# The scaling of the next expert's gathered tokens, behind the Silu of the expert in front

## The chip, the cores and the metric

The kernel runs on one core of one Trainium2 chip. The metric is the device time of one execution in microseconds (us). Before the change it is 2817.28 us, the median of three runs (2815.06 to 2818.99). In what follows PE is TensorE, ACT the scalar engine, DVE VectorE, POOL GpSimd and SP SyncE; each works through its own list of instructions in order.

## The reference

One layer of an encoder: a mixer (windowed attention heads beside mLSTM heads), and behind it a routed mixture of 16 experts, each with the 128 tokens that it chooses among 1024. Only the mixture is touched here:

```python
def expert_choice_moe(h, w_router, w_gate, w_up, w_down):
    cap = CAPACITY_FACTOR * S // N_EXPERTS                 # 2 * 1024 // 16 = 128
    aff = jax.nn.softmax((h @ w_router).astype(jnp.float32), axis=-1)
    gates, idx = lax.top_k(jnp.swapaxes(aff, 1, 2), cap)
    xe = jax.vmap(lambda hb, ib: hb[ib])(h, idx)
    hid = jax.nn.silu(jnp.einsum('becd,edf->becf', xe, w_gate)) * jnp.einsum('becd,edf->becf', xe, w_up)
    ye = jnp.einsum('becf,efd->becd', hid, w_down) * gates[..., None].astype(h.dtype)
    ...
h2 = rms_norm(x) * (1 + sc2) + sh2
x = x + g2 * expert_choice_moe(h2, w_router, w_gate, w_up, w_down)
```

The model is 2048 wide and an expert 1024. All is float32.

## The kernel before

The experts run one after the other, e = 0 to 15, in the last two fifths of the execution. The kernel keeps the residual stream without its norm in HBM (x1p_d). So an expert's tokens are gathered by row (L1288), multiplied by 1/rms of their row (L1312, the scaling of which the change speaks: four pieces of 128x512 on ACT), transposed on PE in four groups of four 128x128 blocks (L1325), and given scale and shift of their column as they leave PSUM (L1334, four pieces per group into xtmp). Float32 accuracy is had from three products of fp32r: every operand is split into a rounded part and a rest. For tokens these are xh (L1337, ACT) and xl (L1338, DVE), for weights ehi (L1353, ACT) and elo (L1359, DVE).

Weights come in chunks of 1 MB over SP's queue, two blocks of 128x1024 in each. For every block ACT makes ehi (four buffers), DVE elo (three buffers), and PE does six matmuls of 128x512 (L419 with ehi, L420 with elo, L421 with the tokens' rest). An expert has 48 blocks: 16 of the gate matrix (g0 to g15), 16 of up (u0 to u15), 16 of down (d0 to d15). From expert 1 on they run in this order: g4 to g15 of expert e, u0 to u15 of e, g0 to g3 of expert e+1, d0 to d15 of e. The tokens of e+1 are made beside that: their transposes' groups 0 to 2 are issued from the up part on, group 3 behind g1. Group 0 is the operand of g0 to g3, group 1 that of g4 to g7, and so on.

Between gate and up stands the Silu (`gated`, L1385), which writes the first half of tile y (one buffer; the scatter of the expert before reads it). The product with up (`hidden`, L1391, DVE) fills the second half, is transposed (`hidden_T`, L1402) and split into hT (L1405, L1406). `down` scales the results into y (L1427) and scatters them with addition into the output (L1429, POOL).

The order on each engine isn't written out by hand alone. The code is written in one order, `issue_after` holds an instruction behind another, and a scheduler with a model of the times places what it may place. The step `prep` of expert e+1 (one-hot of the slots, positions, gather, 1/rms, scaling) is a generator that runs beside the gate part of expert e; nothing but data ties its scaling to a place in ACT's list.

Of the kernel before, what the change touches and what calls it, by code (L numbers as in the profile page):

```python
# [14 lines left out]
AF = mybir.ActivationFunctionType  # L15
# [71 lines left out]
def tile_kernel(ctx: ExitStack, tc: tile.TileContext, x, c, w_ada, b_ada, w_in, b_gates, q_gain, k_gain, sink,  # L87
                m_gain, w_out, w_router, w_gate, w_up, w_down, cosT, sinT, ident_in, near, after, out):
    nc = tc.nc
# [41 lines left out]
    def bank(tag="s", pool=None, dt=F32):  # L131
        pool = pool or (psA if tag == "acc" else psB)
        return pool.tile([128, 512], dt, name=tag, tag=tag)
# [787 lines left out]
    def order(e, w):  # L921
        return MIXED if e + w == 0 else PLAIN
# [349 lines left out]
    def prep(e, p):  # L1272
        oh = mo_p.tile([128, NT, 128], BF, name="oh")
        nc.vector.tensor_tensor(oh, iot[:, None, :].to_broadcast([128, NT, 128]),  # L1274
                                slot[:, :, e:e + 1].to_broadcast([128, NT, 128]), OP.is_equal)
        pm = bank("t")
        for i in range(NT):
            if e:
                nc.tensor.matmul(pm[:, 0:2], oh[:, i], place[:, i], start=i == 0, stop=i == NT - 1)
                continue  # L1280
            for j in range(2):
                nc.tensor.matmul(pm[:, 0:1], oh[:, i], place[:, i, j:j + 1], start=i + j == 0, stop=i + j == NT)
        mt = mo_p.tile([128, 12], F32, name="mt", bufs=3)
        idx = mo_p.tile([128, 1], I32, name="idx", bufs=3)
        xg = mo_p.tile([128, D], F32, name="xg")

        def gather(to, rows, at):
            return nc.gpsimd.indirect_dma_start(out=to, out_offset=None, in_=rows,  # L1288
                                                in_offset=bass.IndirectOffsetOnAxis(ap=at[:, :1], axis=0))

        if e:
            nc.vector.tensor_copy(mt[:, 0:2], pm[:, 0:2])
            p["at"] = nc.vector.tensor_add(idx, mt[:, 0:1], mt[:, 1:2])
            p["fetch"] = gather(xg, x1p_d, idx)
        else:

            for q in FIRST_Q:
                at = mo_p.tile([128, 1], I32, name=f"idx{q}")
                nc.vector.tensor_scalar(at, pm[:, 0:1], 4.0, float(q), op0=OP.mult, op1=OP.add)
                p["fetch"] = gather(xg[:, q * 512:(q + 1) * 512], x1p_d.rearrange("t (q d) -> (t q) d", q=4), at)  # L1300
            p["at"] = nc.vector.tensor_copy(idx, pm[:, 0:1])
        yield
        pv = bank("t")
        for i in range(NT):
            nc.tensor.matmul(pv[:, 0:6], oh[:, i], info[:, i, e], start=i == 0, stop=i == NT - 1)
        nc.vector.tensor_reduce(mt[:, 9:11], pv[:, 0:6].rearrange("p (a b) -> p a b", a=2), axis=AX.X, op=OP.add)
        for i, q in enumerate(FIRST_Q if e == 0 else range(4)):
            xq = xg[:, q * 512:(q + 1) * 512]
            if e == 0 and i % 2:
                nc.vector.tensor_scalar(xq, xq, mt[:, 10:11], None, op0=OP.mult)  # L1310
            else:
                nc.scalar.mul(xq, xq, mt[:, 10:11])  # L1312
        p.update(mt=mt, idx=idx, xg=xg)
        yield

    def tokens_T(p, after=None, first=False):
        p["xh"], p["xl"], p["tmp"] = {}, {}, {}
        for q in FIRST_Q if first else range(4):
            xh = mo_p.tile([128, 4, 128], F32R, name=f"xh{q}")
            xl = mo_p.tile([128, 4, 128], F32R, name=f"xl{q}")  # L1320
            ps = bank("t")
            tmp = mo_p.tile([128, 512], F32, name="xtmp", bufs=2)
            with tc.issue_after(after.ins) if after else nullcontext():
                for b in range(4):
                    nc.tensor.transpose(ps[:, b * 128:(b + 1) * 128],  # L1325
                                        p["xg"][:, (4 * q + b) * 128:(4 * q + b + 1) * 128], ident)
            for b in range(4):
                k = 4 * q + b
                bs = slice(b * 128, (b + 1) * 128)
                if first and b % 2:  # L1330
                    nc.vector.tensor_scalar(tmp[:, bs], ps[:, bs], sc2x[:, k:k + 1], sh2x[:, k:k + 1],
                                            op0=OP.mult, op1=OP.add)
                else:
                    nc.scalar.activation(tmp[:, bs], ps[:, bs], AF.Identity, scale=sc2x[:, k:k + 1],  # L1334
                                         bias=sh2x[:, k:k + 1])
            t3 = tmp.rearrange("p (k n) -> p k n", k=4)
            nc.scalar.copy(xh, t3)  # L1337
            p["made"] = nc.vector.tensor_sub(xl, t3, xh)  # L1338
            p["xh"][q], p["xl"][q], p["tmp"][q] = xh, xl, tmp
            yield  # L1340
# [23 lines left out]
    def rows(e, p, w, cc, half, side):  # L1364

        if w not in p["acc"]:
            p["acc"][w] = [bank("acc") for _ in range(2)]
        acc, (first, last) = p["acc"][w], (order(e, w)[0], order(e, w)[-1])

        direct = e == 0 and (w, cc) in DIRECT  # L1370
        for j, hi, lo in chunk(e, w, cc, half, direct):
            start, stop = (cc, half) == first and j % 2 == 0, (cc, half) == last and j % 2 == 1
            for q in range(2):
                qs = slice(q * 512, (q + 1) * 512)
                if direct:
                    p["last"] = nc.tensor.matmul(acc[q], p["tmp"][cc][:, j * 128:(j + 1) * 128], hi[:, qs],
                                                 start=start, stop=stop)
                    continue
                p["last"] = mm3(acc[q], p["xh"][cc][:, j], p["xl"][cc][:, j], hi[:, qs], lo[:, qs], start, stop)
            side.step()  # L1380

    def gated(p):
        yt = p["y"] = mo_p.tile([128, D], F32, name="y", tag="y")
        for q in range(2):
            nc.scalar.activation(yt[:, q * 512:(q + 1) * 512], p["acc"][0][q], AF.Silu)  # L1385

    def hidden(p):
        yt, p["hid"] = p["y"], []
        for q in range(2):
            hid = yt[:, 1024 + q * 512:1024 + (q + 1) * 512]  # L1390
            nc.vector.tensor_mul(hid.rearrange("t (j p) -> t p j", j=4),  # L1391
                                 p["acc"][1][q].rearrange("t (p j) -> t p j", j=4),
                                 yt[:, q * 512:(q + 1) * 512].rearrange("t (p j) -> t p j", j=4))
            p["hid"].append(hid)
# [38 lines left out]
    first, side = Filler(), Filler()  # L1433
    nc.vector.tensor_reduce(slot[:, :, 0], cnt, axis=AX.X, op=OP.add)
    first.add(prep(0, P[0]))
    first.drain()
    first.add(tokens_T(P[0], first=True))
    first.drain()
    run(select(tp))
    for e in range(16):  # L1440
        p, nxt = P[e], P[e + 1] if e < 15 else None
        if nxt:
            side.add(prep(e + 1, nxt))
        for cc, half in order(e, 0):
            if e < 2 or cc:
                rows(e, p, 0, cc, half, side)
        gated(p)
        if e == 0:
            for cc, half in order(e, 1):
                rows(e, p, 1, cc, half, side)  # L1450
            side.drain()
            side.add(tokens_T(nxt, p["last"]))
            hidden(p)
            ht = hidden_T(p)
            for _ in range(2):
                side.step()
                next(ht)
            down(e, p, side)
            side.drain()
            continue  # L1460
        side.drain()

        turn = tokens_T(nxt) if nxt else iter(())
        for cc in range(4):
            for half in range(2):
                rows(e, p, 1, cc, half, side)
                if half == 0 and cc and nxt:
                    with tc.issue_after(used.ins):
                        next(turn)
            used = p["last"]  # L1470
        hidden(p)
        ht = hidden_T(p)
        if nxt:
            mid = Filler()
            mid.add(iter(()))
            rows(e + 1, nxt, 0, 0, 0, mid)
            with tc.issue_after(nxt["last"].ins):
                next(ht)
                next(ht)
                next(turn)  # L1480
            rows(e + 1, nxt, 0, 0, 1, mid)
        else:
            next(ht)
            next(ht)
        down(e, p, side)
# [45 lines left out]
```

## Time and profile before

| what | value |
|---|---|
| median of three runs | 2817.28 us |
| the profiled execution, and its span | 2817.95 us, 2816.24 us |
| PE busy | 2657.9 us (94%) |
| DVE busy | 2112.9 us (75%) |
| ACT busy | 1564.6 us (56%) |
| granted PE clock, mean | 0.974 |

The busy shares are means over the whole program; the experts are a stage of their own from about 1600 us on. The clock is a share of 2.4 GHz, so that 0.50 is the level of 1.2 GHz. The span is what the trace covers, the execution's time is a little longer.

### The profile page before, as it was taken

The numbers are of one execution on the slowest core, as the hardware profiler recorded it, in microseconds if no ns is written. First come the engines' busy times: TensorE is split into PE (matmuls) and PEld (weight loads), VectorE is DVE, ScalarE is ACT, GpSimd is POOL, SyncE is SP. The second block draws the span as 40 slices with busy tenths as digits, with TensorE's granted clock in tenths as the row PEclk, the third lists the DMA queues.
The fourth block names the chain that finished last, engine by engine and source line by source line (L and its number), as shares of the span: only waits on it lengthen the run. The fifth ranks groups of instructions, "written<-read, shape, count | busy, mean of one in ns | idle before, by whom it ended". The sixth has DMA issues, their size and how long they took to land. (4 is left out here: it accounts for less than half of the span.)

```text
span 2816.2 us, 36979 instructions
## 1 busy us (share of the span) xinstructions
PE 2657.9 (94%) x12392; PEld 2139.0 (76%) x12392; DVE 2112.9 (75%) x3507; ACT 1564.6 (56%) x2585; POOL 363.5 (13%) x311
## 2 busy tenths in 40 slices
PE   7998899999999999999999788999999999999997
PEld 6776787777777787777888566787777777777776
DVE  7777666666666665666745787899999889999886
ACT  6213332333343423333445457788888888888885
POOL 0000232000000003333444501100000000000000
PEclk9999999999999999999999899999999999999999
DMA  8874535555665556655497568999999999999993
GB/s 297 270 247 117 163 83 190 170 171 173 209 187 157 172 178 240 217 207 203 168 319 263 200 238 327 354 362 385 385 381 383 374 382 380 385 385 377 385 359 128
DMA packets 269559, 744.35 MB, mean 264 GB/s; under 512 B 29244, under 2 KB 83240, under 8 KB 232504
## 3 DMA queue, kind: packets, MB, share of 16 engines
q1 hardware_dynamic: 249192, 684.36, 67.6%
q0 software_dynamic: 4976, 33.64, 4.7%
q10 hardware_dynamic: 15200, 24.00, 2.3%
q8 instruction: 97, 1.59, 0.2%
q14 instruction: 94, 0.77, 0.1%
HBM read 672.01 MB, written 69.90 MB: 263 GB/s over the span
## 5 line engine op out<-in xcount | busy, mean ns | idle before, releaser
L1359 DVE TENSOR_TENSOR elo<-ew,ehi 128x1024 fp32r<-128x1024 f32 x432 | 507.6, 1220 | 49.1 <-ACT ehi L1353 35.9
L1353 ACT CAST ehi<-ew 128x1024 fp32r<-128x1024 f32 x432 | 445.1, 1059 | 89.9 <-PE acc L421 56.7
L1359 DVE TENSOR_TENSOR elo<-quad,ehi 128x1024 fp32r<-128x1024 f32 x324 | 380.9, 1219 | 51.9 <-ACT ehi L1353 43.6
L420 PE MATMUL acc<-elo,xh 128*128 128x512 f32 x1008 | 402.1, 399 | 9.7 <-DVE elo L1359 8.8
L421 PE MATMUL acc<-ehi,xl 128*128 128x512 f32 x1008 | 396.4, 393 | 0.0
L1353 ACT CAST ehi<-quad 128x1024 fp32r<-128x1024 f32 x324 | 335.1, 1059 | 72.0 <-PE acc L421 45.2
L419 PE MATMUL acc<-quad,w_hi 128*128 128x512 f32 x896 | 363.7, 407 | 7.3 <-ACT w_hi L388 4.1
L421 PE MATMUL acc<-quad,w_lo 128*128 128x512 f32 x896 | 357.8, 402 | 2.7 <-DVE w_lo L389 2.7
L420 PE MATMUL acc<-quad,w_hi 128*128 128x512 f32 x896 | 359.7, 401 | 0.0
L209 DVE SCALAR_TENSOR_TENSOR ada_acc<-ada_w,csil,ada_acc 128x512 f32<-128x512 f32 x360 | 273.3, 760 | 85.8 <-DMA ada_w<-in_w_ada_dram 82.3
L419 PE MATMUL acc<-ehi,xh 128*128 128x512 f32 x1008 | 322.8, 399 | 13.9 <-ACT ehi L1353 13.9
L388 ACT ACTIVATE w_hi<-w_raw,sc1p 128x128 fp32r<-128x128 f32 (+2 forms) x368 | 161.6, 491 | 312.8 <-PE acc L420 173.6
L420 PE MATMUL acc<-w_lo,quad 128*128 128x512 f32 x768 | 311.5, 406 | 6.7 <-DVE w_lo L378 5.5
L421 PE MATMUL acc<-w_hi,quad 128*128 128x512 f32 x768 | 306.1, 399 | 0.0
L419 PE MATMUL acc<-w_hi,quad 128*128 128x512 f32 x768 | 297.2, 414 | 6.6 <-ACT ev L731 4.9
L772 POOL TENSOR_TENSOR w_raw<-w_raw,quad 128x512 f32<-128x512 f32 x136 | 185.0, 1370 | 885.7 <-DMA quad<-mod_d 606.6
L420 PEld LDWEIGHTS acc<-elo,xh 128*128 128x128 f32 x1008 | 190.6, 189 | 63.2 <-DVE elo L1359 22.3
L419 PEld LDWEIGHTS acc<-ehi,xh 128*128 128x128 f32 x1008 | 187.0, 190 | 54.0 <-ACT ehi L1353 15.5
L421 PEld LDWEIGHTS acc<-ehi,xl 128*128 128x128 f32 x1008 | 190.7, 189 | 38.9
L389 DVE SCALAR_TENSOR_TENSOR w_lo<-w_raw,sc1p,w_hi 128x128 fp32r<-128x128 f32 (+2 forms) x368 | 172.9, 499 | 60.5 <-ACT w_hi L388 58.5
L419 PEld LDWEIGHTS acc<-quad,w_hi 128*128 128x128 f32 x896 | 172.3, 192 | 45.1 <-ACT w_hi L388 4.3
L398 DVE SCALAR_TENSOR_TENSOR accv<-w_raw,sh,accv 128x256 f32<-128x256 f32 (+1 forms) x210 | 116.8, 556 | 119.1 <-DMA w_raw<-in_w_in_dram 117.4
(390 smaller groups left out, 4235.8 us busy)
## 6 DMA issues: line engine op xcount, KB each, us to landing
ada_w<-in_w_ada_dram SPq DMA_DIRECT2D x192, 512.0 KB, 4.3
ew<-in_w_down_dram SPq DMA_DIRECT2D x74, 1024.0 KB, 13.0
ew<-in_w_up_dram SPq DMA_DIRECT2D x73, 1024.0 KB, 7.5
ew<-in_w_gate_dram SPq DMA_DIRECT2D x72, 1024.0 KB, 8.8
quad<-in_w_up_dram SPq DMA_DIRECT2D x54, 1024.0 KB, 7.6
quad<-in_w_down_dram SPq DMA_DIRECT2D x54, 1024.0 KB, 12.2
quad<-in_w_gate_dram SPq DMA_DIRECT2D x54, 1024.0 KB, 10.1
w_raw<-in_w_in_dram SPq DMA_DIRECT2D x176, 256.0 KB, 3.0
```

Source lines behind the costliest of these rows:

```text
L209: alu.scalar_tensor_tensor(acc, t[:, j], csil[:, k:k + 1], acc, op0=OP.mult, op1=OP.add)
L388: nc.scalar.mul(h, r, s)
L389: nc.vector.scalar_tensor_tensor(l, r, s, h, op0=OP.mult, op1=OP.subtract)
L398: nc.vector.scalar_tensor_tensor(accv, raw[:, j], s, accv, op0=OP.mult, op1=OP.add)
L419: nc.tensor.matmul(ps, ah, bh, start=start, stop=False)
L420: nc.tensor.matmul(ps, ah, bl, start=False, stop=False)
L421: return nc.tensor.matmul(ps, al, bh, start=False, stop=stop)
L772: nc.gpsimd.tensor_mul(raw[:, 0], raw[:, 0], g1b[:, nb * 512:(nb + 1) * 512])
L1353: nc.scalar.copy(hi, raw[:, j])
L1359: nc.vector.tensor_sub(lo, raw[:, j], hi)
```

## The change

The scaling is taken out of `prep` into a function of its own, `arrived`. For experts 0 and 1 it is called where it stood. For experts 2 to 15 it is called in the main loop of the expert in front, between its gate part and its up part, and `issue_after` puts it behind the second of that expert's two Silu instructions.

```diff
         nc.vector.tensor_reduce(mt[:, 9:11], pv[:, 0:6].rearrange("p (a b) -> p a b", a=2), axis=AX.X, op=OP.add)
+        p.update(mt=mt, idx=idx, xg=xg)
+        if e < 2:
+            arrived(e, p)
+        yield
+
+    def arrived(e, p):
+
+        mt, xg = p["mt"], p["xg"]
         for i, q in enumerate(FIRST_Q if e == 0 else range(4)):
             xq = xg[:, q * 512:(q + 1) * 512]
             if e == 0 and i % 2:
                 nc.vector.tensor_scalar(xq, xq, mt[:, 10:11], None, op0=OP.mult)
             else:
                 nc.scalar.mul(xq, xq, mt[:, 10:11])
-        p.update(mt=mt, idx=idx, xg=xg)
-        yield
...
         for q in range(2):
-            nc.scalar.activation(yt[:, q * 512:(q + 1) * 512], p["acc"][0][q], AF.Silu)
+            p["silu"] = nc.scalar.activation(yt[:, q * 512:(q + 1) * 512], p["acc"][0][q], AF.Silu)
...
         side.drain()
+        if nxt:
+
+            with tc.issue_after(p["silu"].ins):
+                arrived(e + 1, nxt)
 
         turn = tokens_T(nxt) if nxt else iter(())
```

The scheduler then places the instructions anew. ACT's list in expert 9, before, from the block u2 on (y<-acc is the Silu, xtmp and xh belong to the tokens of expert 10, the scaling stands outside, ahead of u0):

```order
L1353 CAST ehi<-quad_12543 128x1024 x2
L1312 ACTIVATE xg<-xg,mt 128x512 x4
L1353 CAST ehi<-quad_12543 128x1024 x2
L1353 CAST ehi<-quad_13959 128x1024 x4
L1353 CAST ehi<-ew 128x1024 x2
L1334 ACTIVATE xtmp<-t,sh2x,sc2x 128x128 x4
...
L1337 CAST xh_20245<-xtmp 128x512
L1385 ACTIVATE y<-acc 128x512 x2
L1353 CAST ehi<-ew 128x1024 x2
L1334 ACTIVATE xtmp<-t,sh2x,sc2x 128x128 x4
L1405 CAST hT<-s 128x512 x2
```

The same stretch now, from the last twelve blocks ahead of the Silu (the last two of them are g0 and g1 of expert 10):

```order
L1359 CAST ehi<-ew 128x1024 x12
L1391 ACTIVATE y<-acc 128x512 x2
L1320 ACTIVATE xg<-xg,mt 128x512 x4
L1340 ACTIVATE xtmp<-t,sh2x,sc2x 128x128 x4
L1359 CAST ehi<-ew 128x1024 x2
L1340 ACTIVATE xtmp<-t,sh2x,sc2x 128x128 x4
L1343 CAST xh_20129<-xtmp 128x512
L1343 CAST xh_20187<-xtmp 128x512
L1340 ACTIVATE xtmp<-t,sh2x,sc2x 128x128 x4
L1343 CAST xh_20245<-xtmp 128x512
L1359 CAST ehi<-ew 128x1024 x2
L1411 CAST hT<-s 128x512 x2
```

The Silu has kept its place, behind g1 of the next expert; the scaling has gone behind it, and the token pieces, which were spread over the up part, now follow both.

PE's list at the end of the up part of expert 9, before (xh_19684 is the last token group of expert 9, xh_20129 the first of expert 10; a group of transposes of expert 10 stands four blocks earlier):

```order
L1325 MATMUL t<-ident,xg 128x128 x4
L419 MATMUL acc<-ehi,xh_19684 128x512 x2
...
L420 MATMUL acc<-elo,xh_19684 128x512
L421 MATMUL acc<-ehi,xl_19685 128x512
L419 MATMUL acc<-ehi,xh_20129 128x512
L420 MATMUL acc<-elo,xh_20129 128x512
L421 MATMUL acc<-ehi,xl_20130 128x512
```

And now:

```order
L420 MATMUL acc<-elo,xh_19684 128x512
L421 MATMUL acc<-ehi,xl_19685 128x512
L1331 MATMUL t<-ident,xg 128x128 x12
L419 MATMUL acc<-ehi,xh_20129 128x512
L420 MATMUL acc<-elo,xh_20129 128x512
```

The first three groups of transposes stand between u15 and g0. It is the same in experts 5 to 14. In expert 2 the Silu and the scaling stand behind u4, in expert 3 behind u9, in expert 4 behind u13; in expert 1 behind u2, where the Silu stood before as well, with the scaling behind g9. The lists of SP and POOL are as before.

## Rows read from the trace of the kernel before

**Rows 1.** The page, part 1: busy time of each engine, share of the span.
```profile
PE 2657.9 (94%) x12392; PEld 2139.0 (76%) x12392; DVE 2112.9 (75%) x3507; ACT 1564.6 (56%) x2585; POOL 363.5 (13%) x311
```
**Rows 2.** The page, part 5: group, count, busy, mean ns, idle before and releaser.
```profile
L1359 DVE TENSOR_TENSOR elo<-ew,ehi 128x1024 fp32r<-128x1024 f32 x432 | 507.6, 1220 | 49.1 <-ACT ehi L1353 35.9
```
**Rows 3.** Waits of PE, 1745 to 2820: us in total, times, longest.
```profile
PE s L419 <- DVE hT L1406: 6.5, 9, 0.8
PE acc L419 <- ACT ehi L1353: 3.2, 1, 3.2
```
**Rows 4.** Timeline of POOL: start, us, instruction, count, [idle before <- releaser].
```profile
2021.09 2.30 POOL L1429 DMA_INDIRECT out_dram<-y,idx  x1 [21.28 <-DVE y L1427]
...
2737.93 2.29 POOL L1429 DMA_INDIRECT out_dram<-y,idx  x1 [71.56 <-DVE y L1427]
```
**Rows 5.** Timeline of ACT, gate part of expert 9.
```profile
2315.35 1.05 ACT L1353 CAST ehi<-quad 128x1024 fp32r<-128x1024 f32 x1 [0.30 <-PE acc L421]
2316.71 1.06 ACT L1353 CAST ehi<-quad 128x1024 fp32r<-128x1024 f32 x1 [0.30 <-PE acc L421]
2317.67 2.56 ACT L1312 ACTIVATE xg<-xg,mt 128x512 f32<-128x512 f32 x4
2320.13 4.83 ACT L1353 CAST ehi<-quad 128x1024 fp32r<-128x1024 f32 x5
```
**Rows 6.** Timeline of ACT, end of the up part of expert 9.
```profile
2340.66 1.50 ACT L1334 ACTIVATE xtmp<-t,sh2x,sc2x 128x128 f32<-128x128 f32 x4
2342.04 2.01 ACT L1353 CAST ehi<-ew 128x1024 fp32r<-128x1024 f32 x2
2343.93 0.64 ACT L1337 CAST xh<-xtmp 128x512 fp32r<-128x512 f32 x1
2344.45 1.10 ACT L1385 ACTIVATE y<-acc 128x512 f32<-128x512 f32 x2
2345.42 2.02 ACT L1353 CAST ehi<-ew 128x1024 fp32r<-128x1024 f32 x2
```
**Rows 7.** Timeline of PE in expert 9: transposes of tokens, small matmuls, hidden vectors.
```profile
2339.51 0.60 PE L1325 MATMUL t<-ident,xg 128*128 128x128 f32 x4
2339.86 0.71 PE L419 MATMUL acc<-ehi,xh 128*128 128x512 f32 x2
...
2348.16 0.60 PE L1325 MATMUL t<-ident,xg 128*128 128x128 f32 x4
2348.60 0.34 PE L1279 MATMUL t<-place,oh 128*128 128x2 bf16 x8
2348.80 1.07 PE L1402 MATMUL s<-ident,y 128*128 128x128 f32 x8
2349.63 0.72 PE L419 MATMUL acc<-ehi,xh 128*128 128x512 f32 x2
```
**Rows 8.** Timeline of ACT: the scaling in expert 1, the Silu of expert 2.
```profile
1733.02 2.56 ACT L1312 ACTIVATE xg<-xg,mt 128x512 f32<-128x512 f32 x4 [11.54 <-DMA xg<-x1p_d,idx]
...
1825.52 1.08 ACT L1385 ACTIVATE y<-acc 128x512 f32<-128x512 f32 x2 [5.86 <-DMA out_dram<-y,idx]
```
**Rows 9.** Timeline of PE: first work behind three stops.
```profile
1736.57 1.22 PE L419 MATMUL acc<-ehi,xh 128*128 128x512 f32 x2 [10.74 <-ACT ehi L1353]
...
1827.59 0.73 PE L419 MATMUL acc<-ehi,xh 128*128 128x512 f32 x2 [3.15 <-ACT ehi L1353]
...
1990.27 0.50 PE L420 MATMUL acc<-elo,xh 128*128 128x512 f32 x1 [1.58 <-DVE elo L1359]
```
**Rows 10.** Windows: stretch, length, busy of PE, PEld, DVE, ACT, POOL, PEclk, DMA share, GB/s.
```profile
1730.50:1740.60 10.10, 4.00 (x9) 2.70 (x10) 4.05 (x4) 6.99 (x9) 0.00 (x0) 0.50 0.45 169
...
1829.50:1832.80 3.30, 3.30 (x10) 2.54 (x9) 2.56 (x3) 3.30 (x7) 0.00 (x0) 0.50 1.03 420
1986.00:1996.00 10.00, 8.42 (x49) 6.48 (x49) 10.00 (x13) 8.15 (x13) 0.00 (x0) 1.00 0.99 392
...
2778.40:2785.10 6.70, 6.21 (x14) 4.51 (x15) 5.42 (x6) 4.34 (x5) 0.00 (x0) 0.50 0.00 0
```

## The prediction

> **What bounds the kernel now.** I read the page's first part first: TensorE (PE) is busy for 94% of the span [rows 1]. Then the list of waits, for the stage in which experts 2 to 15 run: PE hardly waits there, 6.5 us in all for the transposed hidden vectors, over nine times, and once 3.2 us for a cast [rows 3]. The GpSimd timeline gives the pace: the scatter of expert 4 is issued at 2021.09, that of expert 14 at 2737.93 [rows 4], so ten experts (5 to 14) take 716.84 us, 71.7 us each. The scalar engine's timeline shows what that is made of: in the gate part it casts one 128x1024 block every 1.36 us (2315.35, 2316.71) and each cast first waits for PE to free one of the four ehi buffers [rows 5]. An expert has 48 such blocks, 48 x 1.36 = 65.3 us, and the rest is transposes and one short wait. So in this stage PE is the bound, and ACT and VectorE (DVE) only have to stay ahead of it. They have little room: a DVE subtraction takes 1.22 us of each 1.36 [rows 2]. The scaling costs nothing where it stands now: its four pieces take 2.46 us of ACT (2317.67 to 2320.13) in a part where ACT waits for PE anyway [rows 5].
>
> **The change part by part.** No instruction is added or removed. What moves is ACT's order, and with it PE's and DVE's.
>
> First, what goes. In expert 1 the scaling for expert 2 stood inside the gate part, and ACT waited 11.54 us there for the gather; PE stood still for 10.74 us behind it [rows 8, 9]. With the scaling behind the Silu of expert 1 the gather has long landed. After that stall PE's clock was at 0.50, the 1.2 GHz level, until 1740.6, that is 4.0 us after work began again at 1736.57 [rows 9, 10], worth half of it, 2.0 us. Gone: 12.7 us. What is late next: Silu 0.97, scaling 2.46, cast 0.95 and subtraction 1.22 [rows 2, 5, 6] are 5.6 us in a row, against three casts already made, 4.1 us of PE work. That costs 1.4. Sum for expert 1: -11.3.
>
> Second, experts 5 to 14, ten times. The order shows that the Silu did not come forward to the end of the gate part: it stays near the end of the up part, where it stood (nobody needs it sooner than the product of gate and up). So the scaling goes back to it, and everything that needs scaled tokens goes behind both: all four transposed blocks of the next expert's tokens. Before, three of the four lay among the up blocks. Now the first matmul of the next expert (block g0, directly behind the up part in PE's order) needs the first of these blocks as its weights, and that has to be made after the last up block. Let T be the moment at which PE ends the up part. With four ehi buffers the cast of g1 starts when the third last up block is done, T - 2.7, and ends at T - 1.6. From there ACT runs without a choice: Silu 0.97 (T - 0.65), scaling 2.46 (T + 1.8), four pieces of the first block with scale and shift 1.38 (T + 3.2), two casts 1.89 (T + 5.1), the second block 1.38 (T + 6.5), the rounding copy xh of the first 0.52 (T + 7.0) [rows 5, 6]. PE has twelve transposes to do in that time, 3 x 0.35 = 1.05 us [rows 7], and else nothing. Before, g0 started at T. The new length of an expert: 65.3 of blocks, 7.0 from T to g0, the fourth group of transposes 0.44, the two sets of eight small matmuls 0.20 each, the eight transposes of the hidden vectors 0.83 [rows 7], some 0.3 for restarts: 74.3 us. Against 71.7 that is +2.6. The sum has no wait for the transposed hidden vectors in it any more: their products are made by T + 2, while PE reaches their matmuls at about T + 14, so the short waits of [rows 3] go.
>
> Third, the clock. The trace shows what such a stop does: after 10.74 us without work the level fell and the slow stretch lasted 4.0 us into the work; after 3.15 us it fell from 1829.5 to 1832.8, all of it in work; after a thin stretch with only eight transposes in expert 15 it was low from 2778.4 to 2785.1; after 1.58 us it did not fall [rows 9, 10]. The new stop is 7 us, thin and with transposes in it. Half of 4.0, 3.3 and 6.7 us are 2.0, 1.65 and 3.35 us; I take their mean, 2.3. Ends: 0 and 3.35. The Trainium skill's "TensorE: Matmul & The Clock Gate", section "HAM oscillation — how this bites in real kernels", says that a stop which comes back in every tile pays the slow restart in every tile. By it the ten experts would pay 23 us more; by the shortest gap in the trace alone they would pay none. The trace of before has no repeated stop of this length; its single ones agree with the rule, down to 3.15 us.
>
> So an expert from 5 to 14 costs 2.6 + 2.3 = 4.9 us more, ten of them 49. What lies beside it: SyncE's and GpSimd's rows stand in the same order, and a longer expert asks less of the DMAs.
>
> Fourth, experts 2 to 4. In expert 2 the Silu waits 5.86 us for the scatter of expert 1, out of the same y tile, and PE stops 3.15 us [rows 8, 9]; the scaling now stands behind that Silu and in front of the next cast, so its 2.46 us lengthen the stop in full: +2.5. In expert 3 Silu and scaling stand behind the tenth up block and two token blocks come in a bunch, but ahead of g0: between nothing and a full stop (4.9), I take 2.5. In expert 4 they stand behind u13, three casts earlier than in the full case, so that some 4 us of the stop are left: 3.5 with the clock, 2 without. Expert 15 has no next expert: 0.
>
> Sum: 49 - 11.3 + 2.5 + 2.5 + 3.5 = +46. The profiled execution took 2817.95 us (span 2816.24 and 1.7 around it), the median of the three runs is 0.7 lower. 2817.95 + 46 - 0.7 = 2863.
>
> **The rivals.**
> *The clock stays up.* The transposes within the stop would have to be enough work. For it: 1.58 us did no harm. Against it: expert 15's thin stretch, with eight of them, did [rows 10]. Then 26 - 11.3 + 2.5 + 2.5 + 2 = +22: 2839.
> *DVE falls behind as well.* Three corrections of token blocks, the hidden vectors' split and the subtractions come in one bunch behind the stop; if one subtraction (1.22 us [rows 2]) per expert is late on top and the clock costs 3.35 each time, and expert 1 gets back only 8 because its Silu waits for the scatter of expert 0: 26 + 33.5 + 12 - 8 + 9 = +72: 2890. For it: DVE's 1.22 of 1.36. Against: PE is late by then itself.
> *Faster: the stop is hidden.* ACT would have to have begun the bunch so early that its 8.6 us from the end of g1's cast to xh fit into the lead. It decides at g0: the lead there is 1.6 us and 1.05 of transposes; it would take some five more ehi buffers than the four. If it held, expert 1's 11.3 would stay and the short waits at the hidden vectors, 6.5 in all, would go, against 5 in experts 2 and 3: 2804. The order on ACT, PE and DVE speaks against it.
> *The change does nothing*, with the stop equal to what is saved: that needs 1.1 us per expert instead of 4.9, less than the 2.6 of the order alone. 2817.
>
> **How the numbers follow.** The forecast gets 0.70, with its own range of 2850 to 2880 (clock between 1.65 and 3.35 each, expert 1 between -8 and -13). The clock that stays up gets 0.15, the late DVE 0.09, the hidden stop 0.03, no effect 0.03. The range reaches down to the second case and up to near the third: 2838 to 2884. About 0.2% (5.6 us) is what a measurement of this kernel can tell from none; faster by more than that 0.03, within 0.03, slower by more 0.94.
>
> **What would show it.** Right: in the timelines of experts 5 to 14 ACT runs Silu, scaling, token pieces back to back around the end of the up part; PE has a stop of about 6 us there, twelve transposes in it, ended by xh or xl; the clock column shows a dip for each of these experts; scatters come 76 to 77 us apart. In expert 1 no wait of ACT for the gather, and its gate part near 16 us. Wrong would be: g0 without a stop (then the order on the chip has slack that I do not see), a stop without a dip (then 2839), or scatters 72 us apart.

## The result, and the profile after

The changed kernel takes 2851.4 us, the median of four runs (2851.33 to 2856.05), against 2818.14 us before in the same job: ratio 1.0129, 95% interval 1.0116 to 1.0142. The profiled execution took 2851.4 us too, 33.5 more than that of before. Of all runs of this study two took several times as long as the others of their kernel (13198 us, one of e6, and 6178 us, one of before beside e8), and they are left out of the medians and ratios below. The lines named below are those of the changed kernel, six more than in the rows ahead: L1320 is the scaling, L1340 the token pieces, L1343 xh, L1359 the casts, L1391 the Silu, L1435 the scatter.

Two lines of the page, the busy times and the granted clock in 40 slices; they answer to [rows 1]:

```profile
PE 2672.0 (94%) x12392; PEld 2155.5 (76%) x12392; DVE 2130.6 (75%) x3507; ACT 1582.7 (56%) x2585; POOL 371.2 (13%) x311
...
PEclk9998999999999999999999899999999999999999
```

The instructions are the same in number, and so is PE's share; from the page one could not tell what went wrong. The list of PE's waits from 1740 to 2850 tells more (us in total, times, longest):

```profile
PE acc L419 <- ACT xh L1343: 30.5, 11, 3.1
PE t L1331 <- ACT xtmp L1340: 22.8, 11, 3.8
...
PE s L419 <- DVE hT L1412: 1.0, 1, 1.0
```

In [rows 3] PE hardly waited. Now there are two new waits, each eleven times, once for every expert from 4 to 14, and both for ACT: 53 us in all. The nine short waits for hT have become one. POOL's timeline gives the pace again:

```profile
1791.53 2.33 POOL L1435 DMA_INDIRECT out_dram<-y,idx  x1 [22.56 <-DVE y L1433]
...
1910.87 11.49 POOL L1288 DMA_INDIRECT xg<-x1p_d,idx  x1 [45.76 <-ACT ehi L1359]
...
2009.91 2.30 POOL L1435 DMA_INDIRECT out_dram<-y,idx  x1 [21.20 <-DVE y L1433]
...
2776.85 2.29 POOL L1435 DMA_INDIRECT out_dram<-y,idx  x1 [74.22 <-DVE y L1433]
```

From the scatter of expert 4 (2009.91) to that of expert 14 (2776.85) it is 766.94 us, 76.7 for each expert, where [rows 4] gave 71.7. The first two rows, the scatter of expert 1 and the gather for expert 5, matter further down. ACT's timeline shows expert 1, expert 2 and the end of the up part of expert 9:

```profile
1732.60 1.05 ACT L1359 CAST ehi<-ew 128x1024 fp32r<-128x1024 f32 x1 [0.30 <-PE acc L421]
1733.73 1.09 ACT L1391 ACTIVATE y<-acc 128x512 f32<-128x512 f32 x2
1734.70 2.55 ACT L1320 ACTIVATE xg<-xg,mt 128x512 f32<-128x512 f32 x4
...
1807.39 1.07 ACT L1391 ACTIVATE y<-acc 128x512 f32<-128x512 f32 x2
1808.35 2.56 ACT L1320 ACTIVATE xg<-xg,mt 128x512 f32<-128x512 f32 x4
...
2349.33 1.05 ACT L1359 CAST ehi<-ew 128x1024 fp32r<-128x1024 f32 x1 [0.30 <-PE acc L421]
2350.29 1.07 ACT L1391 ACTIVATE y<-acc 128x512 f32<-128x512 f32 x2
2351.25 2.55 ACT L1320 ACTIVATE xg<-xg,mt 128x512 f32<-128x512 f32 x4
2353.70 1.50 ACT L1340 ACTIVATE xtmp<-t,sh2x,sc2x 128x128 f32<-128x128 f32 x4
2355.07 2.01 ACT L1359 CAST ehi<-ew 128x1024 fp32r<-128x1024 f32 x2
2356.95 1.53 ACT L1340 ACTIVATE xtmp<-t,sh2x,sc2x 128x128 f32<-128x128 f32 x4
2358.33 1.18 ACT L1343 CAST xh<-xtmp 128x512 fp32r<-128x512 f32 x2
```

In expert 1 the Silu and the scaling follow the casts without a wait (the 11.54 us of [rows 8] are gone). In expert 2 the Silu doesn't wait for a scatter either. In expert 9, from 2349.33 on, no row but the first has an idle time in brackets: ACT works without a pause for 10 us, and everything that g0 needs is at the end of that row of work. In [rows 6] a token group lies between casts of the up part, and two more stood ahead of it in the same way. PE's timeline in the same place:

```profile
2351.62 0.39 PE L421 MATMUL acc<-ehi,xl 128*128 128x512 f32 x1
2352.03 1.27 PE L1331 MATMUL t<-ident,xg 128*128 128x128 f32 x8
2355.25 0.84 PE L1331 MATMUL t<-ident,xg 128*128 128x128 f32 x4 [1.96 <-ACT xtmp L1340]
2359.04 0.79 PE L419 MATMUL acc<-ehi,xh 128*128 128x512 f32 x1 [2.95 <-ACT xh L1343]
```

The up part ends at 2351.85 (T; u15 begins at 2350.49 and takes 1.36), g0 begins at 2359.04: T + 7.2, and between them lie twelve transposes. The windows of the clock, in expert 9 and in the last expert (columns as in [rows 10]):

```profile
2355.77:2362.55 6.78, 3.83 (x11) 2.79 (x10) 3.91 (x5) 6.40 (x14) 0.00 (x0) 0.51 0.73 302
...
2812.00:2819.00 7.00, 5.00 (x25) 3.82 (x25) 4.47 (x6) 2.79 (x5) 0.00 (x0) 1.00 0.00 0
```

In expert 9 the granted clock is at the 1.2 GHz level for 6.8 us, and the first 3.4 us of the work from g0 on fall into that. Each expert from 5 to 14 has such a stretch of 6.83 us, expert 4 one of 3.41. In expert 15, where before the clock was low for 6.8 us [rows 10], it now stays at 1.00.

By stage, each expert from the start of its block g4 to that of the next (counted in PE's order, six matmuls to a block; us):

| stage | before | after | moved | predicted |
|---|---|---|---|---|
| expert 1 | 83.3 | 71.2 | -12.1 | -11.3 |
| expert 2 | 75.6 | 71.3 | -4.3 | +2.5 |
| expert 3 | 70.6 | 72.3 | +1.7 | +2.5 |
| expert 4 | 71.2 | 74.8 | +3.6 | +3.5 |
| experts 5 to 14 | 718.4 | 767.0 | +48.5 | +49 |
| expert 15 to the end | 79.8 | 75.9 | -3.9 | 0 |
| sum | | | +33.5 | +46 |

### The profile page after: what moved, and what is told of

Its sections match the earlier page's. It is cut to its first block, busy times and chain, and to the rows that moved or that the text cites. A ratio compares the mean times of both kernels' runs of the same rounds, so it can differ in the third digit from the quotient of the medians.

```text
span 2849.7 us, 37029 instructions
## 1 busy us (share of the span) xinstructions
PE 2672.0 (94%) x12392; PEld 2155.5 (76%) x12392; DVE 2130.6 (75%) x3507; ACT 1582.7 (56%) x2585; POOL 371.2 (13%) x311
## 4 chain that ended last, share of the span: by engine, by line
PE 63%; DMA 14%; DVE 11%; ACT 6%; issue 5%; POOL 0%; SPq 0%; POOLq 0%; DVEq 0%; ACTq 0%
PE acc L420 16%; PE acc L419 16%; PE acc L421 16%; DMA ada_w<-in_w_ada_dram 4%; DMA w_raw<-in_w_in_dram 4%; DVE ada_acc L209 2%; DVE w_lo L389 2%; PE s L420 2%; PE s L419 2%; PE s L421 2%; ACT ehi L1359 2%; ACT xtmp L1340 1%; DVE accv L398 1%; DMA ew<-in_w_down_dram 1%; DMA mE<-M_d 1%
## 5 line engine op out<-in xcount | busy, mean ns | idle before, releaser
L1365 DVE TENSOR_TENSOR elo<-ew,ehi 128x1024 fp32r<-128x1024 f32 x432 | 514.9, 1220 | 61.1 <-ACT ehi L1359 25.7
L1359 ACT CAST ehi<-ew 128x1024 fp32r<-128x1024 f32 x432 | 450.8, 1058 | 127.8 <-PE acc L421 94.0
L1359 ACT CAST ehi<-quad 128x1024 fp32r<-128x1024 f32 x324 | 338.5, 1057 | 95.6 <-PE acc L421 70.0
L419 PE MATMUL acc<-ehi,xh 128*128 128x512 f32 x1008 | 331.1, 404 | 30.7 <-ACT xh L1343 30.5
L419 PEld LDWEIGHTS acc<-ehi,xh 128*128 128x128 f32 x1008 | 193.9, 193 | 74.6 <-ACT xh L1343 33.7
```

The costliest lines, as they stand in the source:

```text
L419: nc.tensor.matmul(ps, ah, bh, start=start, stop=False)
L1359: nc.scalar.copy(hi, raw[:, j])
L1365: nc.vector.tensor_sub(lo, raw[:, j], hi)
```

## The experiments

The start of expert 1's g4 lies between 1717.0 and 1727.9 us in the profiled executions of this study, though the edits below concern only what comes behind it. That is 11 us, or 0.4% of the time, so totals of different kernels compare only to about that; the lengths of experts repeat far better (each of experts 5 to 14 took 71.68 us before and 71.70 when that kernel was profiled again), and the verdicts rest on them. Each ratio is taken to runs of before in the same job, whose median lay between 2818 and 2822 us. The table has them for all kernels; "5 to 14" is a tenth of the time between the scatters of experts 4 and 14, "low" the number of experts among these ten in which the granted clock fell.

| kernel | median us | ratio to before [95%] | expert 1 | expert 2 | 5 to 14 | low | 15 to the end |
|---|---|---|---|---|---|---|---|
| before | 2818.14 | 1 | 83.3 | 75.6 | 71.7 | 1 | 79.8 |
| the change | 2851.40 | 1.0129 [1.0116, 1.0142] | 71.2 | 71.3 | 76.7 | 10 | 75.9 |
| e1, Silu ahead of u4 | 2802.62 | 0.9925 [0.9908, 0.9943] | 71.4 | 72.1 | 71.4 | 0 | 77.4 |
| e8, ahead of u8 | 2805.58 | 0.9952 [0.9935, 0.9969] | 71.3 | 71.3 | 72.2 | 0 | 75.8 |
| e5, ahead of u12 | 2823.70 | 1.0006 [0.9994, 1.0019] | 71.3 | 71.3 | 73.7 | 5 | 75.8 |
| e3, stop filled | 2840.65 | 1.0069 [1.0051, 1.0087] | 71.3 | 71.3 | 75.1 | 0 | 77.2 |
| e2, expert 2 alone | 2811.61 | 0.9974 [0.9960, 0.9989] | 71.5 | 76.9 | 71.7 | 0 | 79.5 |
| e6, experts 2 and 3 | 2805.06 | 0.9939 [0.9919, 0.9958] | 71.3 | 71.3 | 71.8 | 1 | 79.9 |
| e7, before, Silu ahead of u4 | 2884.83 | 1.0213 [1.0186, 1.0239] | 83.7 | 77.4 | 76.7 | 10 | 77.5 |

**e1: the change, and the Silu held in its place.** The theory (A): the scaling behind the Silu costs nothing in itself; the loss comes from where the scheduler then puts both, at the end of the up part. So the cast of block u4 is held behind the Silu, which puts Silu and scaling at the head of the up part. `PIN` names the block.

```diff
+PIN = (1, 0)
...
-            nc.scalar.copy(hi, raw[:, j])
+            held = e and w == 1 and j == 0 and (cc, half) == PIN
+            with tc.issue_after(P[e]["silu"].ins) if held else nullcontext():
+                nc.scalar.copy(hi, raw[:, j])
```

> The changed kernel with one more hold: from expert 1 on, the cast of block u4 stands behind the Silu, so that Silu and scaling come at u3/u4 and not at g1 of the next expert. Theory A (the loss is the place of the Silu: the scaling, the transposes and the token blocks come in a bunch right ahead of g0, which needs them): the stop of 7.2 us at g0 and the clock's dip go in experts 4 to 14, an expert is 71.5 to 72.5 us again (76.9 in the changed kernel, 71.8 before), and the gain in expert 1 (12 us) stays: 2805 to 2815 us. Rival B (3.4 us of ACT for Silu and scaling in one piece hold up the casts wherever they stand): stops of like size move into the up part: 2840 us or more.

Measured: 2802.62 us. ACT's timeline, where PE has just ended the gate part of expert 9:

```profile
2313.99 1.06 ACT L1362 CAST ehi<-quad 128x1024 fp32r<-128x1024 f32 x1 [0.76 <-PE acc L422]
2314.95 1.07 ACT L1394 ACTIVATE y<-acc 128x512 f32<-128x512 f32 x2
2315.92 2.55 ACT L1321 ACTIVATE xg<-xg,mt 128x512 f32<-128x512 f32 x4
2318.37 1.98 ACT L1362 CAST ehi<-quad 128x1024 fp32r<-128x1024 f32 x2
```

The Silu begins 22.8 us before the up part of this expert ends (at 2337.7, where g0 begins), in the changed kernel 1.6 us before. The ten experts take 71.4 us each, and none has a low clock. B is out. The total is a little under what A expected; gains of 3.5 us in expert 2 and 2.4 in the last expert were not in that sum. It is faster than both kernels: added up, its experts 1 to 15 take 21 us less than before.

**e8 and e5: the same with u8 and with u12.** Only the block in `PIN` is another (against e1).

```diff
-PIN = (1, 0)
+PIN = (2, 0)        # e8;  (3, 0) in e5
```

> The changed kernel with the cast of block u8 held behind the Silu from expert 1 on; a third point between u4 (71.45 us for each of experts 5 to 14) and u12 (73.7 us). Theory A (the loss grows with what the scalar engine still has to do for the tokens when the up part ends): two token groups are done by u12 as the order has it, the third ends with the up part, g0 starts without a stop and the clock stays up in these experts; what is left is the third group's correction and the wait for the hidden vectors at d0, 0 to 1 us: 71.4 to 72.5 us each, 2802 to 2814 us in all. Rival B (the bunch itself, two token groups in one row between two casts, is what costs, wherever it stands): 73 us or more each, 2817 us and above.

> The changed kernel with the cast of block u12 (not u4) held behind the Silu, so in experts 2 to 14 the Silu runs at the latest after u11 instead of after the whole up part. Theory A (the loss is the distance from the Silu's place to the end of the up part): the Silu and the scaling run about six casts, 8 us, earlier than in the changed kernel, so two of the four transpose groups fall inside the up part, T to g0 shrinks from 7.2 us to 2.5 to 4 us, PE stops less than 2 us, and the ten experts cost 72.0 to 74.0 us each, between 71.45 (held at u4) and 76.7 (not held): 2808 to 2830 us in all. Rival B (any work on the scalar engine between two casts of the up part costs what it costs behind it): the periods stay at 76 or more, 2845 us and above. Rival C (what counts is only whether the clock falls): periods as with u4, within 0.3 us, as soon as no dip shows: 2800 to 2806 us.

Measured: 72.2 us each with u8, 73.7 with u12. Both lie where A put them; e8's and e5's rivals are out (B in both: 73 and 76 or more; C in e5: four of the five experts with the clock up took 72.9 to 73.0, not 71.4). PE's waits, first of u8 from 2000 to 2730:

```profile
PE acc L421 <- DVE elo L1368: 10.1, 22, 0.8
PE s L421 <- DVE elo L1368: 4.9, 6, 0.8
PE s L420 <- DVE hT L1415: 2.6, 2, 1.3
```

and of u12 from 2010 to 2750:

```profile
PE s L420 <- DVE hT L1415: 14.4, 11, 3.2
PE acc L421 <- DVE elo L1368: 8.7, 9, 1.8
PE acc L422 <- DVE xl L1345: 1.9, 1, 1.9
```

With u8 PE waits mostly for DVE's subtractions, in many stops of at most 0.8 us. Two details of my expectation for u12 failed: I expected g0 at T + 2.5 to T + 4, with stops under 2 us, and it began no later than T + 1.2 in each of the ten, while the longest stop is one of 3.2 us further on, at d0, for the hidden vectors. The bunch on ACT had moved the stop, not only shortened it. So the price is not a matter of g0 alone: 71.4, 72.2, 73.7 and 76.7 us for a Silu behind the casts of u3, u7, u11 and g1.

**e3: the stop filled with useless matmuls.** How much of the +4.9 is the clock? In experts 5 to 14 PE does six extra matmuls of 128x512 within the stop, two behind the second group of transposes and four behind the third, into a bank that nobody reads. `turned` holds the last transpose of each group.

```diff
+WARM = 2, 4
...
+                    turned.append(nxt["turned"])
...
+        if nxt and 5 <= e:
+            warm = bank("s")
+            for after_, n in ((turned[1], WARM[0]), (turned[2], WARM[1])):
+                with tc.issue_after(after_.ins):
+                    for _ in range(n):
+                        nc.tensor.matmul(warm, ident, g2b[0][:, 0:512], start=True, stop=True)
```

> The changed kernel with six matmuls of no use (128x512 float32, into a PSUM bank that is free there) in PE's list in the stop at g0 of experts 5 to 14, two behind the second group of transposes and four behind the third. They add work and take nothing away. Theory A (part of the loss is PE's clock, which falls in the stop and stays low some 4 us into the work): no dip in these experts, 1.7 to 2.3 us less in each: 2829 to 2835 us. Rival C (the low clock lies beside ACT's and DVE's own chain and costs nothing): 2851, or more by what the six matmuls take.

Measured: 2840.65 us, between the two. PE's timeline in expert 9:

```profile
2352.34 1.27 PE L1332 MATMUL t<-ident,xg 128*128 128x128 f32 x8
2353.44 1.88 PE L1488 MATMUL s<-g2b,ident 128*128 128x512 f32 x4
2355.56 0.66 PE L1332 MATMUL t<-ident,xg 128*128 128x128 f32 x4 [0.24 <-ACT xtmp L1341]
2356.05 3.60 PE L1488 MATMUL s<-g2b,ident 128*128 128x512 f32 x8
2359.35 0.53 PE L420 MATMUL acc<-ehi,xh 128*128 128x512 f32 x1
```

Each of the six float32 matmuls counts as two instructions (4 and 8). The clock over the same stretch:

```profile
2351.00:2359.30 8.30, 8.05 (x30) 4.07 (x28) 4.18 (x4) 8.30 (x18) 0.00 (x0) 1.00 1.01 421
2356.00:2362.80 6.80, 6.80 (x28) 4.27 (x26) 3.94 (x5) 6.50 (x14) 0.00 (x0) 1.00 0.73 304
```

The up part ends at 2352.16 and g0 begins at 2359.35, T + 7.2 as without them: in this expert the filling cost nothing, and the clock stayed at 1.00. In six experts (6, 9 to 12, 14) g0 came no later than in the changed kernel; these took 74.6 us in the mean, and 76.8 in the changed kernel. So the clock is 2.2 us per expert in the mean, and the order 2.8 (74.6 against 71.8 for the same six before). It is not the same in each: filling the stop gave back 1.5 us in expert 9 and 2.5 in expert 10, where the low stretch of the changed kernel began 3.5 us and 1.2 us ahead of g0. In the four others the filling made g0 late, by 0.7 to 1.6 us, which is why the ten gained only 16 us. C, for which the clock is nothing, is out; A holds in size, but its total did not count on fillings that get in the way.

**e2 and e6: the change for expert 2 alone, and for experts 2 and 3.** All other experts have the scaling where it was before.

```diff
-        if e < 2:
+        if e != 2:                      # e6: if e not in (2, 3)
+            arrived(e, p)
...
-        if nxt:
+        if e == 1:                      # e6: if e in (1, 2)
+            with tc.issue_after(p["silu"].ins):
+                arrived(e + 1, nxt)
```

> Only the tokens of expert 2 are scaled behind the Silu (of expert 1); for experts 3 to 15 the code of before. The scheduler gives these experts another order than before all the same: Silu and scaling stand behind u7 in experts 5 to 14. Theory A: with them behind u7 the token blocks are made in time for g0, so there is no stop there; expert 1 keeps its 12 us: 2803 to 2815 us. Rival B: about 2840, as Silu and scaling stand in one piece here too.

> Only the scaling of experts 2 and 3 stands behind the Silu in front of it; the code of before for all others. Question: what freed expert 2 in the changed kernel. Before and with expert 2's scaling alone behind the Silu, the scatter of expert 1 took GpSimd 10.28 us and the Silu of expert 2 waited for it; in the changed kernel it took 2.33 us. Theory D (the place of expert 3's scaling, through the order of the work around it, decides): the scatter of expert 1 takes 2.3 us, expert 2's period is 71 to 72.5 us instead of 76.9, and the total is 2802 to 2810 us. Rival E (it hangs on what stands further back in the program, experts 4 to 15): the scatter takes 10 us again, expert 2's period is 75 to 77 us, total 2808 to 2815 us.

Measured: in both, expert 1 has its gain and experts 5 to 14 take what they took before. Expert 2 differs: 76.9 and 71.3 us. POOL's timeline has the reason, in e2

```profile
1795.02 10.28 POOL L1435 DMA_INDIRECT out_dram<-y,idx  x1 [23.25 <-DVE y L1433]
```

and in e6

```profile
1798.43 2.33 POOL L1435 DMA_INDIRECT out_dram<-y,idx  x1 [22.60 <-DVE y L1433]
```

It is the scatter of expert 1. Where it kept POOL busy for 10.28 us, the Silu of expert 2 waited for it, in e2

```profile
1815.94 1.08 ACT L1391 ACTIVATE y<-acc 128x512 f32<-128x512 f32 x2 [6.35 <-DMA out_dram<-y,idx]
```

D holds, E falls: with expert 3's scaling ahead of that Silu the scatter is slow; with it behind, it isn't.

**e4: the kernel before, unchanged, profiled once more.** Is the slow scatter chance?

> The kernel before, unchanged, for the 10.28 us that POOL took for the scatter of expert 1 (2.3 in later ones) and the wait of the Silu of expert 2 behind it. If this belongs to the program, the same scatter is slow again and the Silu waits some 6 us. If it varies from run to run, another gather or scatter is slow here, or none, and the 4.3 us that expert 2 gained in the changed kernel are not the change's. 2815 to 2820 us.

Measured: 2819.09 us, with the same row in POOL's timeline:

```profile
1805.15 10.28 POOL L1429 DMA_INDIRECT out_dram<-y,idx  x1 [24.03 <-DVE y L1427]
```

It is not chance from one execution to the next: it was 10.28 us in both profiles of before, in e2 and in e7, where expert 3's scaling stands ahead of the Silu, and 2.33 in the changed kernel, e1, e3, e5, e6 and e8, where it stands behind.

**e7: the scaling where it was, the Silu held ahead of u4.** The kernel before, with the hold of e1 alone; the edge of the change isn't there.

```diff
+PIN = (1, 0)
...
-            nc.scalar.copy(hi, raw[:, j])
+            held = e and w == 1 and j == 0 and (cc, half) == PIN
+            with tc.issue_after(P[e]["silu"].ins) if held else nullcontext():
+                nc.scalar.copy(hi, raw[:, j])
...
-            nc.scalar.activation(yt[:, q * 512:(q + 1) * 512], p["acc"][0][q], AF.Silu)
+            p["silu"] = nc.scalar.activation(yt[:, q * 512:(q + 1) * 512], p["acc"][0][q], AF.Silu)
```

> The kernel before, with its scaling where it was (in the gate part, in front of the Silu), and the cast of block u4 held behind the Silu from expert 1 on. It tells what the edge of the change is worth when the place of the Silu is fixed in both. Theory A (the edge itself costs nothing, the drift of the Silu behind it was the loss, and its gain is the gather of expert 2 and the scatter of expert 1): expert 1 takes 83 us again with the ACT wait of 11 to 12 us for the gather, expert 2 takes 75 to 76 us or 71 to 72 us, experts 5 to 14 take 71.4 us each: 2812 to 2821 us, 10 to 19 us over the kernel that is held at u4 with the edge. Rival (the edge costs by itself even where the Silu is held, and pays nothing): 2803 us or less.

Measured: 2884.83 us, slower than any other, which neither theory expected. ACT's timeline in expert 9:

```profile
2366.90 1.06 ACT L1356 CAST ehi<-quad 128x1024 fp32r<-128x1024 f32 x1 [0.76 <-PE acc L422]
2372.33 1.51 ACT L1335 ACTIVATE xtmp<-t,sh2x,sc2x 128x128 f32<-128x128 f32 x4 [4.37 <-PE t L1326]
2373.87 0.62 ACT L1338 CAST xh<-xtmp 128x512 fp32r<-128x512 f32 x1
2374.39 1.08 ACT L1388 ACTIVATE y<-acc 128x512 f32<-128x512 f32 x2
```

With the tokens scaled early, the scheduler put the first token group in front of the held Silu. Its transposes stand in PE's list behind blocks that PE has still to do, so ACT waits 4.37 us with the Silu and the cast of u4 behind it, and PE then stops for the cast:

```profile
2376.45 1.03 PE L420 MATMUL acc<-ehi,xh 128*128 128x512 f32 x2 [4.16 <-ACT ehi L1356]
```

All ten experts have a low clock again, by another stop. So this run doesn't tell what the edge alone is worth in experts 5 to 14; experts 1 and 2 took 83.7 and 77.4 us, as expected of a scaling in front. What it does tell: at u4, holding the Silu paid only together with the edge, which keeps token work behind it.

## Why the prediction was right, and where it was wrong

2863 us were predicted and 2851.4 measured, within the range and with the right sign, though only just above the lower end of the forecast's own 2850 to 2880. By its steps:

*Expert 1, -11.3.* Right: -12.1, with no wait for the gather. Both of its terms are there: the gate part fell from 29.6 to 16.5 us (12.7 were predicted to go), and the up part grew from 23.4 to 24.7 (predicted 1.4).

*Experts 5 to 14, the order, +2.6 each.* Right: 2.8 by e3. The times that the prediction counted from T are in ACT's timeline almost to the tenth, with T at 2351.85: scaling from T - 0.6, its end T + 1.85, first token group T + 3.2, two casts T + 5.1, second group T + 6.5, g0 at T + 7.2 (predicted 7.0). The short waits for hT went as said [rows 3]. That this is the cause, and not the scaling's new neighbour as such, is shown by e1, e8 and e5, where the same two steps stand earlier and the price falls with the distance.

*The clock, +2.3 each.* Right in the mean: 2.2 by e3, with a stretch of low clock in each of the ten experts, and none in e3. The working had 3.3 to 6.7 us of work at the low clock; each stretch was 6.83 us long and began within the stop, so that 3.4 us of it lay behind the start of g0 in expert 9 and 5.6 in expert 10. That a mean of three unlike cases hit the mean of these was partly luck. The rule weighed there, of the Trainium skill's "TensorE: Matmul & The Clock Gate", section "HAM oscillation — how this bites in real kernels", holds in these ten. The transposes within the stop did not keep the clock up; the rival that hoped for that is out.

*Expert 2, +2.5.* Wrong: -4.3. The step said that the Silu of expert 2 would wait 5.86 us for the scatter of expert 1 as before, with the scaling's 2.46 on top. That took over a wait of before as if it were fixed. The wait of [rows 8] was made by a POOL instruction of 10.28 us, and e2 and e6 show that it goes when expert 3's scaling stands behind that Silu. Why POOL is slower in the one order is not shown: beside the scatter of 10.28 us in before and that of 2.33 us in the change alike, DVE made its subtractions without a pause.

*Experts 3 and 4, +2.5 and +3.5.* +1.7 and +3.6. In expert 4 the mechanism is the predicted one, a shorter stop (g0 some 4.4 us behind T) and a low stretch of 3.41 us. In expert 3 there is no stop at g0 and no low clock; the 2.5, a value taken between two bounds, was of the right size by luck.

*Expert 15, 0.* Wrong: -3.9. "No next expert, so nothing" overlooked that the order behind the Silu moved there too. Before, ACT stood idle ahead of the first hT, and the casts of d0 and d1 came behind it:

```profile
2776.84 0.59 ACT L1405 CAST hT<-s 128x512 fp32r<-128x512 f32 x1 [4.79 <-PE s L1402]
2777.32 1.99 ACT L1353 CAST ehi<-quad 128x1024 fp32r<-128x1024 f32 x2
```

Now the casts come first:

```profile
2811.31 1.99 ACT L1359 CAST ehi<-quad 128x1024 fp32r<-128x1024 f32 x2
2813.52 0.59 ACT L1411 CAST hT<-s 128x512 fp32r<-128x512 f32 x1 [0.22 <-PE s L1408]
```

From the start of d0 to the last matmul it is 22.1 us, 25.6 before; the gate part is 0.7 us shorter, and the rest is 0.4 longer. How much of the 3.6 us at d0 and behind it is the clock, which was low for 6.8 us before and now stays up, isn't settled: half of the 6.2 us that PE was busy in that stretch would be 3.1, but in e2 the clock was low there for only 3.41 us and the same part still took 25.1, which speaks for a price of the late casts by themselves. The kernels with before's code in expert 15 (before, e2, e6) need 79.5 to 80.0 us to the end, the others 75.8 to 77.5. No run changed that order alone, so for the last expert this is read from traces and not tested.

The two misses, -6.8 and -3.9, are 10.7 of the 12.5 us between the predicted +46 and the measured +33.5; the term that carried the forecast was right in both of its halves. That the two pulled the same way is what brought the time near the end of the range.

## What to carry to other kernels

An ordering edge doesn't say where its first end goes. Before holding work behind an instruction, look up where the scheduler puts that instruction now and who pulls it there; then count, engine by engine, from the last buffer that comes free to the first matmul that needs the result. And a wait in the trace of before is only as fixed as the order that made it: ask for each one that a sum carries over what would have to stay for it to stay.

## What the runs showed of the hardware that was not expected

- From expert 1 on one indirect DMA on POOL takes 1.0 to 2.4 us of the engine or 9 to 13 us, and in the one program that was profiled twice it was the same ones that were slow both times. Between programs it differs: the gather for expert 5 took 11.49 us in the change (the second of POOL's rows above) and 1.14 us in e6. It cost time where somebody waited: for the y tile in expert 2, and in expert 1 of before, where the wait of 11.54 us [rows 8] ended when the gather below landed, 19.2 us after its issue. In the change this gather kept POOL busy for 12.80 us, and nobody waited. What decides it stays open.

```profile
1713.76 10.53 POOL L1288 DMA_INDIRECT xg<-x1p_d,idx  x1 [0.30 <-issue]
```

- A filling of matmuls that reads old data and writes to a free bank kept the clock at 1.00 through a stop of 7.2 us and gave back 2.2 us in the mean of the six experts where it was not itself in the way.
- In e5 the same kernel has experts with and without a low clock: after a wait of 3.16 us at d0 in expert 10 it was at 0.50, after 1.46 us at the same place in expert 9 it was not, as [rows 9, 10] had it with 3.15 and 1.58. But the length of one wait doesn't decide it: in the same run the clock fell in experts 8 and 13, where the longest wait was one of 1.78 us, and stayed up in expert 14 after one of 2.04.
